# Weaving the attention of three mixers with projections and gates: one encoder kernel before and after

## The chip, the cores and the metric

The kernel runs on one core of a Trainium2 chip. The metric is the time of one execution in microseconds (us) on the device. A core has five engines that run side by side, each with a queue of its own that it works through in order: PE (TensorE, matrix products; its weight loads are shown as PEld), DVE (VectorE), ACT (ScalarE), POOL (GpSimd) and SP (SyncE, which here only issues DMAs). Matrix products go from SBUF into PSUM, and the other engines take them from there.

## The reference

Two layers work on 272 tokens (16 meta tokens and a grid of 4 rows by 64 columns) of width 1024. Each layer is a SwiGLU, a step with three mixers, and a second SwiGLU, all with residuals. The change concerns the step with the mixers:

```python
qa, ka, va, qb, kb, vb, qc, kc, vc, gates = jnp.split(n @ w_in, offsets, axis=-1)
...
oa = window_sink_attention(apply_rope(heads(qa, A_Q_HEADS), ang), apply_rope(heads(ka, A_KV_HEADS), ang),
                           heads(va, A_KV_HEADS), sink)
ob = neighbourhood_attention(heads(qb, B_HEADS), heads(kb, B_HEADS), heads(vb, B_HEADS), rpb)
qc = apply_axial_rope(rms_norm(heads(qc, C_Q_HEADS), qn), row, col)
kc = apply_axial_rope(rms_norm(heads(kc, C_KV_HEADS), kn), row, col)
oc = dense_block_attention(qc, kc, heads(vc, C_KV_HEADS))
branches = jnp.stack([oa, ob, oc], axis=2)
up = jnp.einsum('blnc,ncd->blnd', branches, w_branch)
g = jax.nn.sigmoid(gates.reshape(B, L, N_BRANCH, D_MODEL))
return jnp.sum(g * up, axis=2) @ w_out
```

So there are three attentions A, B and C with eight heads of 64 each (A within a window and with a sink logit, B within a neighbourhood on the grid, C over all tokens with normalised queries and keys), and each result goes through a branch matrix and is scaled by a gate, which is one more projection of the same normalised input. In the last layer only the 256 grid tokens are wanted, so that layer has no queries for the meta tokens.

## The kernel before

**Weights.** Activations lie transposed: 128 channels in the partitions, tokens along the free dimension. Every weight matrix comes in units of 512 x 256 numbers. SP issues the load of a unit into `raw` (four buffers), ACT rounds it into `hi` (L227), and DVE, or POOL for every third unit in the mixers, computes the rest `lo` (L228). `mm` (L271 to L273) multiplies each 128 x 128 block three times (hi by hi, hi by lo, lo by hi) into an accumulator `acc`, a PSUM tile of which there are two. A projection of 256 columns takes two units and 48 products; a branch takes one unit and 24.

**The mixers as written.** `mixer` writes its steps one behind the other: projections of B (values, keys, queries), then all of B's attention (`neighbourhood`), then A's keys and queries with their rotary turn (`rope_a`), then all of A's attention (`grouped` with br 0), then C's keys and queries (L721 to L763), then C's attention (`grouped` with br 2), then twelve gate steps in a loop (L769: four each for branch B, A and C), then the output projection.

**One attention.** An attention goes through two blocks of 128 queries, and each block through two halves of four heads. A half is a chain. PE computes four score tiles into PSUM tiles `s` (L468 or L604; three buffers). DVE adds masks and takes the maximum, and ACT the exponent (`scores`, L388 and L390, or L393 to L395). DVE normalises the four together (L407, L408, L481). PE turns the weights by transposes into `s` again (L487 or L612), ACT copies them out (L490 or L615), and after two halves `weighted` (L418, L423) multiplies them with the values into `pv`. After the two blocks, in the layer that has meta queries, the 16 meta tokens' queries go through the same chain once more (L502 to L534).

**The order on an engine.** The framework that builds the program orders each engine's instructions itself. The written order is their priority: an instruction that is ready and stands earlier goes first, and a later one may move ahead of it while it waits. A tile comes from a tag with so many buffers, and must wait until one is free. The tag `sm` of small tiles has 14 buffers. It serves A's and C's maxima `mx`, sums `den` and sink terms `e` (the `e` of `add_sinks` is first written at L400), and also C's norms: `rq`, `rqv` and `t24` of 24 columns and `sm` at L751. `rqv` is first written by the copies at L749, which take the sums of squares of C's queries out of the accumulator in which the projection of those queries lay (L739 and L746). Only after these copies, and in the first layer those of L757, is that accumulator free for another projection.

Of the kernel before, what the change touches and what calls it, by code (L numbers as in the profile page):

```python
# [17 lines left out]
D = 1024  # L18
# [73 lines left out]
def encoder_kernel(ctx: ExitStack, tc: tile.TileContext, x, meta_tokens, ffn1_norm, ffn1_w_in, ffn1_w_out,  # L92
# [359 lines left out]
    def grouped(br, q, kk, vt, oh, ol, masks, mask_m, sinks, sink_m, rq, meta_queries):  # L452

        v01, vm, v16 = v_prep(vt, meta_queries)
# [3 lines left out]
        for qi in range(2):  # L458
            pv = bank("pv")
            pm = sb.tile([128, 8, META], F32, name=nm("pm"), tag="pm", bufs=2)  # L460
            pmt = sb.tile([128, 128], F32, name=nm("pmt"), tag="pmt", bufs=2)
            both = []
            for half in range(2):
                p, mx, den = wide(), small(), small()
                for i in range(4):
                    t, g = 2 * half + i // 2, i % 2
                    s = bank("s", 3)[:, :T]
                    PE.matmul(s, q[g * HD:(g + 1) * HD, t, qi * 128:(qi + 1) * 128], kk[g * HD:(g + 1) * HD, :],  # L468
                              start=True, stop=True)
                    if rq is None:  # L470
                        scores(p, i, s, den, mx, masks[qi], nsink[:, 4 * g + t:4 * g + t + 1], None)
                    else:
                        c = qi * 8 + 2 * t + g
                        scores(p, i, s, den, mx, None, None, rq[:, c:c + 1])
                if rq is None:
                    e = small()
                    DVE.tensor_copy(e[:, :4].rearrange("p (t g) -> p t g", g=2),
                                    sinks.rearrange("p (g t) -> p t g", g=2)[:, 2 * half:2 * half + 2, :])
                    add_sinks(den, mx, e[:, :4], 4)
                normalise(p[:, :, :GRID], den)  # L480
                DVE.tensor_tensor(pm[:, 4 * half:4 * half + 4], p[:, :, GRID:],  # L481
                                  den[:, :4, None].to_broadcast([128, 4, META]), op=ALU.mult)
                for t2 in range(2):
                    pt = bank("s", 3)
                    for g in range(2):
                        for kt in range(2):
                            PE.transpose(pt[:, (2 * g + kt) * 128:(2 * g + kt + 1) * 128],  # L487
                                         p[:, 2 * t2 + g, kt * 128:(kt + 1) * 128], ident)
                    pts = sb.tile([128, 512], F32, name=nm("pts"), tag="pts", bufs=PTS)
                    ACT.copy(pts, pt)  # L490
                    both.append(pts)
            pt = bank("s", 3)
            PE.transpose(pt[:, :128], pm.rearrange("p a b -> p (a b)"), ident)
            DVE.tensor_copy(pmt, pt[:, :128])
            weighted(pv, vm, pmt, both, lambda t, g, kt, pts: (
                v01[:, kt, g * HD:(g + 1) * HD], pts[:, (2 * g + kt) * 128:(2 * g + kt + 1) * 128]))
            sl = (slice(None), slice(4 * br, 4 * br + 4), slice(qi * 128, (qi + 1) * 128))
            split(oh[sl], ol[sl], pv.rearrange("p (t q) -> p t q", t=4))
        if not meta_queries:
            return  # L500

        qm = sb.tile([128, 4, META], F32, name=nm("qm"), tag="qm", bufs=1)  # L502
        DVE.tensor_copy(qm, q[:, :, GRID:])
        qm = qm.rearrange("p t j -> p (t j)")
        s = bank("s", 3)[:, :T]
        for g in range(2):
            PE.matmul(s[g * HD:(g + 1) * HD, :], qm[g * HD:(g + 1) * HD, :], kk[g * HD:(g + 1) * HD, :],
                      start=True, stop=True)
        p = sb.tile([128, 1, T], F32, name=nm("pq"), tag="pq", bufs=1)
        den, mx = small(), small()  # L510
        if rq is None:
            nsink = small()
            DVE.tensor_scalar(nsink[:, :1], sink_m, -1.0, None, op0=ALU.mult)
        scores(p, 0, s, den, mx, mask_m, nsink[:, :1] if rq is None else None, None if rq is None else rq[:, 16:17])
        if rq is None:
            add_sinks(den, mx, sink_m, 1)
        normalise(p[:, 0:1, :], den)
# [32 lines left out]
    def neighbourhood(biases, q, kb, vb, oh, ol, meta_queries):  # L550
# [45 lines left out]
        for qi in range(2):  # L596
            pv = bank("pv")
            both = []
            for half in range(2):
                p, mx, den = wide(), small(), small()  # L600
                for i in range(4):
                    t, g = 2 * half + i // 2, i % 2
                    s = bank("s", 3)[:, :KB]
                    PE.matmul(s, q[g * HD:(g + 1) * HD, t, qi * 128:(qi + 1) * 128],  # L604
                              kb[g * HD:(g + 1) * HD, t, qi, :], start=True, stop=True)
                    scores(p, i, s, den, mx, biases[qi][:, 2 * t + g, :], 3.0e38, None)
                normalise(p[:, :, :KB], den)
                for t2 in range(2):
                    pt = bank("s", 3)
                    for g in range(2):  # L610
                        for kt in range(2):
                            PE.transpose(pt[:KH, (2 * g + kt) * 128:(2 * g + kt + 1) * 128],  # L612
                                         p[:, 2 * t2 + g, kt * KH:(kt + 1) * KH], ident)
                    pts = sb.tile([128, 512], F32, name=nm("pts"), tag="pts", bufs=PTS)
                    ACT.copy(pts[:KH].rearrange("p (b q) -> p b q", b=4), backwards(pt[:KH], 4))  # L615
                    both.append(pts)
# [4 lines left out]
            split(oh[sl], ol[sl], pv.rearrange("p (t q) -> p t q", t=4))  # L621


    def mixer(l, norm, nxt, last):
# [48 lines left out]
        neighbourhood(biases, qb, kb, vb, oh, ol, not last)  # L673


        tab = scr()
        DVE.tensor_tensor(tab[:, 0, :], C("cos_a"), r, op=ALU.mult)
        DVE.tensor_tensor(tab[:, 1, :], C("sin_a"), r, op=ALU.mult)
# [10 lines left out]
        qa = q_tile()  # L689
        a = proj(plain(w, 0, 8, A_KV))  # L690
        ka, va = kv_tile("k"), kv_tile("v")
        rope_a(ka[:, None, :], a[:, 0:1, :T], 1)
        DVE.tensor_tensor(va, a[:, 1, :T], r, op=ALU.mult)
        for half in range(2):
            a = proj(head_pairs(w, A_Q, half), n_out)
            rope_a(qa[:, 2 * half:2 * half + 2, :n_out], a[:, :, :n_out], 2)
        sink_m = None
        if not last:
            t8 = small()
            DVE.tensor_tensor(t8, sink[:, l, :], C("head_of"), op=ALU.mult)  # L700
            sink_m = small()
            DVE.tensor_reduce(sink_m[:, :1], t8, axis=AX, op=ALU.add)
            sink_m = sink_m[:, :1]
        grouped(0, qa, ka, va, oh, ol, (C("mask_a0"), C("mask_a1")), C("mask_am"), sink[:, l, :], sink_m, None,
                not last)


        rq = small((128, 24))
# [12 lines left out]
        a = proj(plain(w, 0, 8, C_KV))  # L721
        kc, vc = kv_tile("k"), kv_tile("v")
        u = scr()
        DVE.tensor_tensor(u[:, 0, :], a[:, 0, :T], r, op=ALU.mult)
        DVE.tensor_tensor(vc, a[:, 1, :T], r, op=ALU.mult)
        ACT.activation(u[:, 1, :], u[:, 0, :], AF.Square)
        for i in range(2):
            PE.matmul(a[:, i, T:T + 136], heads, u[:, 1, i * 136:(i + 1) * 136], start=True, stop=True)
        v2 = scr()
        rk = scr()  # L730
        DVE.tensor_scalar(v2[:, 0, :].rearrange("p (a b) -> p a b", a=2), a[:, :, T:T + 136], 1.0 / HD, EPS,
                          op0=ALU.mult, op1=ALU.add)
        rsqrt(rk[:, 0, :], v2[:, 0, :], v2[:, 1, :])
        rope_c(kc[:, None, :], u[:, 0:1, :], 2 + l, 1)
        DVE.tensor_tensor(kc, kc, rk[:, 0, :], op=ALU.mult)
        qc = q_tile()
        rqv = small((128, 24))
        for half in range(2):
# [9 lines left out]
            for qi in range(2):  # L748
                DVE.tensor_copy(rqv[:, qi * 8 + half * 4:qi * 8 + half * 4 + 4], a[:, 0, T + qi * 4:T + qi * 4 + 4])  # L749
            if not last:  # L750
                sm = small((128, 32))  # L751
                DVE.tensor_copy(sm.rearrange("p (t j) -> p t j", t=2), sq[:, :, GRID:])
                for g in range(2):
# [122 lines left out]
```

## Time and profile before

| what | value |
|---|---|
| time, median of three runs | 1374.4 us (1373.92 to 1376.08) |
| profiled execution: its time | 1374.38 us |
| profiled execution: first to last instruction | 1372.6 us |
| mean granted clock of PE | 0.985 |
| instructions shown as work on PE | 10703 |
| bytes read from memory | 214.78 MB |

The profile is of one execution. Its page gives busy times by engine, the busy shares in 40 slices, the chain of waits that ended last, and the costliest groups of instructions. Further views give stretches of the span with busy time and granted clock (windows), instructions in order of time (the timeline; "x8" is a run of eight like ones, and what stands in brackets at the end is the idle time of the engine just before it, with the instruction that ended it), and who waited for whom (waits). The first layer's mixers take about 225 to 460 us of the span, and the second's about 930 to 1130 us.

### The profile page before, as it was taken

To read this page: it belongs to the slowest core of one execution; us is meant where nothing else is said; L and a number is where in the kernel's file an instruction comes from. 1 tells how busy PE (TensorE), PEld (TensorE's weight loads), DVE (VectorE), ACT (ScalarE), POOL (GpSimd) and SP (SyncE) were. 2 spreads that over 40 slices of the span, in tenths; PEclk is the share of its full clock that TensorE was granted. 3 is DMA by queue.
4 is the path that set the end of the run, shared out by engine and by line. 5 is a ranking of instruction groups with operands and counts; after the bars stand their busy time and mean duration, and the time that the engine had idled before them with its cause. 6 is when DMAs were issued, how large, how long until landed. Compare 5 with 4: busy or idle time off the path is not lost.

```text
span 1372.6 us, 25976 instructions
## 1 busy us (share of the span) xinstructions
PE 1341.0 (98%) x10703; PEld 1295.2 (94%) x10703; DVE 898.5 (65%) x1326; ACT 651.6 (47%) x933; POOL 168.3 (12%) x99
## 2 busy tenths in 40 slices
PE   8999999997999999999999999999999999999997
PEld 8999999986789999999999999999888999999997
DVE  7665668687555577655677656676797556865663
ACT  6443444464454455434445434454565445543444
POOL 1000003231013330000000000022321242000000
PEclk9999999997899999999999999999999999999999
DMA  7665555432125666555555555555232466665652
GB/s 225 196 191 170 180 178 185 139 92 64 46 69 172 176 190 193 179 175 179 166 179 178 170 183 170 161 177 169 78 108 79 140 194 188 185 186 190 191 171 77
DMA packets 239010, 217.52 MB, mean 158 GB/s; under 512 B 24804, under 2 KB 237980, under 8 KB 238764
## 3 DMA queue, kind: packets, MB, share of 16 engines
q1 hardware_dynamic: 238540, 215.20, 51.1%
q8 instruction: 84, 1.38, 0.4%
q10 hardware_dynamic: 352, 0.66, 0.1%
q14 instruction: 34, 0.28, 0.1%
HBM read 214.78 MB, written 1.05 MB: 157 GB/s over the span
## 4 chain that ended last, share of the span: by engine, by line
PE 90%; DVE 6%; ACT 1%; issue 1%; DMA 0%; SPq 0%; DVEq 0%; ACTq 0%
PE acc L272 27%; PE acc L273 27%; PE acc L271 27%; PE s L468 2%; PE pv L423 2%; DVE p L408 1%; PE s L487 1%; PE s L604 1%; DVE lo L228 1%; PE pv L418 1%; PE s L612 1%; PE s L326 0%; DMA raw<-in_ffn_w_in_dram 0%; DVE xl L315 0%; DVE p L388 0%
## 5 line engine op out<-in xcount | busy, mean ns | idle before, releaser
L227 ACT CAST hi<-raw 128x1024 fp32r<-128x1024 f32 (+1 forms) x392 | 404.4, 1032 | 573.5 <-PE acc L272 413.3
L272 PE MATMUL acc<-xl,hi 128*128 128x272 f32 (+1 forms) x2176 | 627.5, 288 | 0.6 <-DVE xl L315 0.4
L273 PE MATMUL acc<-xh,lo 128*128 128x272 f32 (+1 forms) x2176 | 624.4, 287 | 0.7 <-DVE lo L228 0.7
L271 PE MATMUL acc<-xh,hi 128*128 128x272 f32 (+1 forms) x2176 | 624.2, 287 | 0.9 <-ACT xh L314 0.9
L228 DVE TENSOR_TENSOR lo<-raw,hi 128x1024 fp32r<-128x1024 f32 (+1 forms) x352 | 430.2, 1223 | 217.0 <-ACT hi L227 216.6
L271 PEld LDWEIGHTS acc<-xh,hi 128*128 128x128 f32 x2176 | 412.7, 190 | 6.1 <-issue 4.6
L272 PEld LDWEIGHTS acc<-xl,hi 128*128 128x128 f32 x2176 | 411.0, 189 | 5.4 <-issue 3.8
L273 PEld LDWEIGHTS acc<-xh,lo 128*128 128x128 f32 x2176 | 411.2, 189 | 4.1 <-issue 3.1
L272 PE MATMUL acc<-hl,hi 128*128 128x272 f32 (+1 forms) x704 | 201.9, 287 | 0.0
L273 PE MATMUL acc<-hh,lo 128*128 128x272 f32 (+1 forms) x704 | 201.1, 286 | 0.0
L271 PE MATMUL acc<-hh,hi 128*128 128x272 f32 (+1 forms) x704 | 200.4, 285 | 0.0
L228 POOL TENSOR_TENSOR lo<-raw,hi 128x1024 fp32r<-128x1024 f32 x40 | 97.9, 2447 | 307.7 <-ACT hi L227 307.7
L271 PEld LDWEIGHTS acc<-hh,hi 128*128 128x128 f32 x704 | 132.7, 189 | 0.1
L273 PEld LDWEIGHTS acc<-hh,lo 128*128 128x128 f32 x704 | 132.3, 188 | 0.0
L272 PEld LDWEIGHTS acc<-hl,hi 128*128 128x128 f32 x704 | 132.2, 188 | 0.0
L321 POOL TENSOR_TENSOR ss<-ss,scr 128x544 f32<-128x544 f32 (+1 forms) x12 | 17.5, 1460 | 600.6 <-ACT scr L318 600.6
L272 PE MATMUL acc<-ol,hi 128*128 128x272 f32 (+1 forms) x192 | 54.8, 286 | 0.0
L271 PE MATMUL acc<-oh,hi 128*128 128x272 f32 (+1 forms) x192 | 54.7, 285 | 0.0
L273 PE MATMUL acc<-oh,lo 128*128 128x272 f32 (+1 forms) x192 | 54.6, 285 | 0.0
L370 DVE TENSOR_TENSOR scr<-acc,scr 128x544 f32<-128x544 f32 (+1 forms) x40 | 28.7, 716 | 31.7 <-PE acc L273 31.6
L280 DVE SCALAR_TENSOR_TENSOR h<-acc,h 128x544 f32<-128x544 f32 (+1 forms) x40 | 28.5, 713 | 28.7 <-PE acc L273 28.5
L367 DVE TENSOR_TENSOR scr<-acc,rstd 128x544 f32<-128x544 f32 (+1 forms) x40 | 28.6, 715 | 26.2 <-PE acc L273 26.2
(228 smaller groups left out, 1322.6 us busy)
## 6 DMA issues: line engine op xcount, KB each, us to landing
raw<-in_ffn_w_in_dram SPq DMA_DIRECT2D x176, 512.0 KB, 3.6
raw<-in_ffn_w_out_dram SPq DMA_DIRECT2D x80, 512.0 KB, 3.4
raw<-in_w_in_dram SPq DMA_DIRECT2D x80, 512.0 KB, 3.7
raw<-in_w_in_dram SPq DMA_DIRECT2D x32, 256.0 KB, 3.2
raw<-in_w_branch_dram SPq DMA_DIRECT2D x32, 256.0 KB, 3.9
raw<-in_w_out_dram SPq DMA_DIRECT2D x16, 512.0 KB, 3.9
raw<-in_ffn_w_out_dram SPq DMA_DIRECT2D x16, 256.0 KB, 2.7
raw<-in_w_branch_dram SPq DMA_DIRECT2D x8, 512.0 KB, 3.4
```

Of the source, the lines that this page charges most:

```text
L227: ACT.copy(hi[:, :n], raw[:, :n])
L228: lo_engine().tensor_tensor(lo[:, :n], raw[:, :n], hi[:, :n].bitcast(F32), op=ALU.subtract)
L271: PE.matmul(o, a, rh, start=k == 0, stop=False)
L272: PE.matmul(o, a, rl, start=False, stop=False)
L273: PE.matmul(o, b, rh, start=False, stop=k == len(rows) - 1)
L280: DVE.scalar_tensor_tensor(hv, a[:, :, :n], 0.5, hv, op0=ALU.mult, op1=ALU.add)
L321: (DVE if j == 3 else POOL).tensor_tensor(ss, ss, dst, op=ALU.add)
L367: DVE.tensor_tensor(g, gate, rb, op=ALU.mult)
L370: DVE.tensor_tensor(g, up, g, op=ALU.mult)
L408: DVE.tensor_tensor(p, p, den[:, :n, None].to_broadcast([128, n, p.shape[2]]), op=ALU.mult)
L423: PE.matmul(pv[g * HD:(g + 1) * HD, t * 128:(t + 1) * 128], a, b, start=vm is None and kt == 0, stop=kt == 1 and (vm is None or t == 3))
L468: PE.matmul(s, q[g * HD:(g + 1) * HD, t, qi * 128:(qi + 1) * 128], kk[g * HD:(g + 1) * HD, :], start=True, stop=True)
```

## The change

`grouped` and `neighbourhood` become generators: after the four scores of a half they stop and let the caller write something else. Each half's turning of the weights, and after the second half the product with the values, is written behind the scores of the next half. The meta queries' scores are written ahead of the last turning. `mixer` puts its other steps into functions (`a_keys`, `a_queries`, `c_keys`, `c_queries`, `gated`) and `weave` writes one of them at each stop: A's keys and queries and C's keys between the halves of B, C's queries and gates of B between those of A, and the remaining gates of B and gates of A between those of C. The order of the projections among themselves, and so of the loads of their weights, is what it was. C's `rq`, `rqv` and `t24`, the meta squares `sqm` and A's `sinkm` get tiles of their own, outside the tag `sm`. The sums of squares of C's meta queries are taken once for both halves, and the copies at L749 are one for both query blocks.

```diff
+        def products(qi, half, pm):
+            p, mx, den = wide(), small(), small()
+            for i in range(4):
...
+            normalise(p[:, :, :GRID], den)
...
+        def turned(p):
...
+        def values(qi, pm, both):
...
+        last = None
+        for qi in range(2):
+            pm = sb.tile([128, 8, META], F32, name=nm("pm"), tag="pm", bufs=2)
+            done = []
+            for half in range(2):
+                p = products(qi, half, pm)
+                if last is not None:
+                    last()
+                yield
+                last = lambda p=p, qi=qi, half=half, pm=pm, done=done: (
+                    done.extend(turned(p)), values(qi, pm, done) if half else None)
+        if meta_queries:
+            p = meta_products()
+        last()
         if not meta_queries:
             return
...
+        yield
         pt = bank("s", 3)
...
-        rq = small((128, 24))
+        rq, rqv, t24 = (sb.tile([128, 24], F32, name=nm(x), tag=x, bufs=1) for x in ("rq", "rqv", "t24"))
+        sqm = sb.tile([128, 4, META], F32, name=nm("sqm"), tag="sqm", bufs=1)
...
-            for qi in range(2):
-                DVE.tensor_copy(rqv[:, qi * 8 + half * 4:qi * 8 + half * 4 + 4], a[:, 0, T + qi * 4:T + qi * 4 + 4])
+            DVE.tensor_copy(rqv[:, :16].rearrange("p (q h c) -> p q h c", q=2, h=2)[:, :, half, :],
+                            a[:, 0, T:T + 8].rearrange("p (q c) -> p q c", q=2))
             if not last:
-                sm = small((128, 32))
-                DVE.tensor_copy(sm.rearrange("p (t j) -> p t j", t=2), sq[:, :, GRID:])
-                for g in range(2):
-                    o = g * HD + half * 32
-                    PE.matmul(a[o:o + 32, 1, T:T + 1], sm[g * HD:(g + 1) * HD, :], ones[g * HD:(g + 1) * HD, :1],
-                              start=True, stop=True)
-                    DVE.tensor_copy(rqv[o:o + 32, 16:17], a[o:o + 32, 1, T:T + 1])
+                DVE.tensor_copy(sqm[:, 2 * half:2 * half + 2, :], sq[:, :, GRID:])
+                if half:
+                    for g in range(2):
+                        rows = slice(g * HD, (g + 1) * HD)
+                        PE.matmul(a[rows, 1, T:T + 1], sqm[rows].rearrange("p t j -> p (t j)"), ones[rows, :1],
+                                  start=True, stop=True)
+                    DVE.tensor_copy(rqv[:, 16:17], a[:, 1, T:T + 1])
...
+        def gated(b, mp):
+            if not tot:
+                tot.extend(qk(4, T) for _ in range(2))
+            if b == 2 and not halves:
+                halves.extend([qk(4, T, dt=F32R) for _ in range(2)] for _ in range(2))
...
+        def weave(attention, others):
+
+            for _ in attention:
+                if others:
+                    others.pop(0)()
+
+        others = [a_keys, lambda: a_queries(0), lambda: a_queries(1), c_keys]
+        weave(neighbourhood(biases, qb, kb, vb, oh, ol, not last), others)
+        others += [lambda: c_queries(0), lambda: c_queries(1)]
+        others += [lambda mp=mp: gated(1, mp) for mp in range(4)]
+        weave(mix_a(), others)
+        others += [lambda mp=mp: gated(0, mp) for mp in range(4)]
+        weave(mix_c(), others)
+        others += [lambda mp=mp: gated(2, mp) for mp in range(4)]
+        for work in others:
+            work()
```

More of the change, by code (lines that the diff above doesn't have):

```diff
@@ new lines, in turned @@
+        def turned(p):
+            both = []
+            for t2 in range(2):
+                pt = bank("s", 3)
+                for g in range(2):
+                    for kt in range(2):
+                        PE.transpose(pt[:, (2 * g + kt) * 128:(2 * g + kt + 1) * 128],
+                                     p[:, 2 * t2 + g, kt * 128:(kt + 1) * 128], ident)
+                pts = sb.tile([128, 512], F32, name=nm("pts"), tag="pts", bufs=PTS)
+                ACT.copy(pts, pt)
+                both.append(pts)
+            return both
@@ L499, in grouped @@
+        last()
         if not meta_queries:
             return
[L502 to L509, printed above, removed]
@@ L595, in neighbourhood @@
             split(oh[sl], ol[sl], pv[:, :4 * META].rearrange("p (t j) -> p t j", t=4))
-        for qi in range(2):
-            pv = bank("pv")
[L598 to L616, printed above, removed]
@@ new lines, in products @@
+        def products(qi, half):
+            p, mx, den = wide(), small(), small()
+            for i in range(4):
+                t, g = 2 * half + i // 2, i % 2
+                s = bank("s", 3)[:, :KB]
+                PE.matmul(s, q[g * HD:(g + 1) * HD, t, qi * 128:(qi + 1) * 128],
+                          kb[g * HD:(g + 1) * HD, t, qi, :], start=True, stop=True)
+                scores(p, i, s, den, mx, biases[qi][:, 2 * t + g, :], 3.0e38, None)
+            normalise(p[:, :, :KB], den)
+            return p
@@ new lines, in turned @@
+        def turned(p):
+            both = []
+            for t2 in range(2):
+                pt = bank("s", 3)
+                for g in range(2):
+                    for kt in range(2):
+                        PE.transpose(pt[:KH, (2 * g + kt) * 128:(2 * g + kt + 1) * 128],
+                                     p[:, 2 * t2 + g, kt * KH:(kt + 1) * KH], ident)
+                pts = sb.tile([128, 512], F32, name=nm("pts"), tag="pts", bufs=PTS)
+                ACT.copy(pts[:KH].rearrange("p (b q) -> p b q", b=4), backwards(pt[:KH], 4))
+                both.append(pts)
+            return both
@@ L617, in neighbourhood, with values @@
+        def values(qi, both):
+            pv = bank("pv")
             weighted(pv, None, None, both, lambda t, g, kt, pts: (
@@ L621, in neighbourhood @@
             split(oh[sl], ol[sl], pv.rearrange("p (t q) -> p t q", t=4))
+        last = None
+        for qi in range(2):
+            done = []
+            for half in range(2):
+                p = products(qi, half)
+                if last is not None:
+                    last()
+                yield
+                last = lambda p=p, qi=qi, half=half, done=done: (
+                    done.extend(turned(p)), values(qi, done) if half else None)
+        last()
     def mixer(l, norm, nxt, last):
@@ L672, in mixer @@
                                   op=ALU.mult)
[L673 to L678, printed above, removed]
+        tab = None
         def rope_a(dst, src, m):
@@ L719, in rope_c, with c_keys, c_queries @@
             DVE.tensor_tensor(dst, dst, t, op=ALU.add)
[L721 to L738, printed above, removed]
+        def c_keys():
+            a = proj(plain(w, 0, 8, C_KV))
+            u = scr()
+            DVE.tensor_tensor(u[:, 0, :], a[:, 0, :T], r, op=ALU.mult)
+            DVE.tensor_tensor(vc, a[:, 1, :T], r, op=ALU.mult)
+            ACT.activation(u[:, 1, :], u[:, 0, :], AF.Square)
+            for i in range(2):
+                PE.matmul(a[:, i, T:T + 136], heads, u[:, 1, i * 136:(i + 1) * 136], start=True, stop=True)
+            v2 = scr()
+            rk = scr()
+            DVE.tensor_scalar(v2[:, 0, :].rearrange("p (a b) -> p a b", a=2), a[:, :, T:T + 136], 1.0 / HD, EPS,
+                              op0=ALU.mult, op1=ALU.add)
+            rsqrt(rk[:, 0, :], v2[:, 0, :], v2[:, 1, :])
+            rope_c(kc[:, None, :], u[:, 0:1, :], 2 + l, 1)
+            DVE.tensor_tensor(kc, kc, rk[:, 0, :], op=ALU.mult)
+        def c_queries(half):
+            if not half:
+                qc[0] = q_tile()
             a = proj(head_pairs(w, C_Q, half), n_out)
@@ L758, in mixer @@
-            rope_c(qc[:, 2 * half:2 * half + 2, :n_out], u, l, 2)
-        nq = 16 if last else 17
-        t24 = small((128, 24))
-        DVE.tensor_scalar(rqv[:, :nq], rqv[:, :nq], 1.0 / HD, EPS, op0=ALU.mult, op1=ALU.add)
-        rsqrt(rq[:, :nq], rqv[:, :nq], t24[:, :nq])
-        DVE.tensor_scalar(rq[:, :nq], rq[:, :nq], 0.125, None, op0=ALU.mult)
-        grouped(2, qc, kc, vc, oh, ol, None, None, None, None, rq, not last)
-        tot = [qk(4, T) for _ in range(2)]
-        mh, ml = ([qk(4, T, dt=F32R) for _ in range(2)] for _ in range(2))
```

157 lines of the change are left out of this document (85 added, 72 removed).

## The prediction

> **What bounds the kernel now.** I read the page first, then PE's work by windows, then the timeline of the one stretch that stands out, then the waits.
>
> ```profile
> span 1372.6 us, 25976 instructions
> ...
> PE 1341.0 (98%) x10703; PEld 1295.2 (94%) x10703; DVE 898.5 (65%) x1326; ACT 651.6 (47%) x933; POOL 168.3 (12%) x99
> ...
> PEclk9999999997899999999999999999999999999999
> ...
> PE 90%; DVE 6%; ACT 1%; issue 1%; DMA 0%; SPq 0%; DVEq 0%; ACTq 0%
> ```
>
> PE is busy for 98% of the span and makes up 90% of the chain that ended last, so only what shortens PE's own time can count. The digits of the clock say where PE was slow: only in the tenth and eleventh slices, 309 to 377 us, which is the first layer's mixers. The windows go around that stretch, and then through the second layer's attention.
>
> ```profile
> 225.00:322.00 97.00, 95.82 (x767) 86.57 (x766) 73.63 (x193) 49.88 (x108) 26.09 (x17) 1.00 0.35 105
> 322.00:366.00 44.00, 33.35 (x182) 26.02 (x180) 22.99 (x74) 14.98 (x34) 4.58 (x2) 0.69 0.15 47
> 366.00:410.00 44.00, 41.66 (x321) 35.03 (x321) 27.60 (x56) 24.12 (x53) 7.45 (x3) 1.00 0.28 85
> ...
> 955.00:1080.00 125.00, 122.77 (x984) 105.23 (x982) 98.16 (x243) 76.02 (x173) 30.70 (x18) 1.00 0.32 97
> ```
>
> The columns are the stretch, its length, then busy time and instructions of PE, PEld, DVE, ACT and POOL, the granted clock, and the DMA share and rate. Before 322 us PE does 767 products in 97 us, 7.9 a microsecond; after 366 us 321 in 44, 7.3; in the second layer 984 in 125, 7.9. Between 322 and 366 us it does 182 in 44, 4.1 a microsecond, at a clock of 0.69, while DVE (23 us) and ACT (15 us) are half idle. So no engine bounds this stretch. The timeline of PE in it:
>
> ```profile
> 324.65 0.28 PE L273 MATMUL acc<-xh,lo 128*128 128x272 f32 x1
> 328.20 1.25 PE L487 MATMUL s<-cst,p 128*128 128x128 f32 x8 [3.27 <-DVE pm L481]
> 329.38 2.17 PE L468 MATMUL s<-k,qk 64*128 64x272 f32 x6
> 331.48 1.87 PE L746 MATMUL acc<-cst,scr 128*128 128x2 f32 x8
> 333.29 1.27 PE L468 MATMUL s<-k,qk 64*128 64x272 f32 x2
> 339.81 1.94 PE L487 MATMUL s<-cst,p 128*128 128x128 f32 x8 [5.25 <-DVE pm L481]
> 341.54 0.42 PE L493 MATMUL s<-cst,pm 128*128 128x128 f32 x1
> 341.89 1.17 PE L507 MATMUL s<-k,qm 64*64 64x272 f32 x2
> 342.98 2.07 PE L418 MATMUL pv<-pmt,vm 128*128 128x128 f32 x8
> 344.99 2.44 PE L423 MATMUL pv<-pts,v 128*64 128x128 f32 x32
> 347.36 0.67 PE L507 MATMUL s<-k,qm 64*64 64x272 f32 x2
> 349.63 0.22 PE L755 MATMUL acc<-ones,sm 64*32 64x1 f32 x2 [1.60 <-DVE sm L752]
> ...
> 355.48 0.59 PE L271 MATMUL acc<-xh,hi 128*128 128x272 f32 x1
> 355.87 0.43 PE L272 MATMUL acc<-xl,hi 128*128 128x272 f32 x1
> 356.10 0.43 PE L273 MATMUL acc<-xh,lo 128*128 128x272 f32 x1
> ```
>
> At 324.65 us the last product of C's query projection starts, and only at 355.48 us the next projection, the first gate's. For 31 us PE has nothing but A's attention, one chain of scores, exponents, turning and values, and the sums of C's squares (L746). It waits for the chain, and its clock drops. L746 between two rows of A's attention shows that the framework already moves C's work ahead of A's. Why then no gates? DVE's rows, with PE's L746 (315.75 and 1015.33) for comparison, the second layer below:
>
> ```profile
> 315.75 0.51 PE L746 MATMUL acc<-cst,scr 128*128 128x2 f32 x4
> ...
> 349.20 0.15 DVE L400 TENSOR_TENSOR sm<-sm,sm 128x1 f32<-128x1 f32 x1
> 349.26 0.22 DVE L749 COPY sm<-acc 128x4 f32<-128x4 f32 x2
> ...
> 351.93 0.17 DVE L757 COPY sm<-acc 32x1 f32<-32x1 f32 x1
> ```
> ```profile
> 1015.33 1.05 PE L746 MATMUL acc<-cst,scr 128*128 128x2 f32 x8
> ...
> 1022.91 0.15 DVE L400 TENSOR_TENSOR sm<-sm,sm 128x4 f32<-128x4 f32 x1
> 1022.99 0.22 DVE L749 COPY sm<-acc 128x4 f32<-128x4 f32 x2
> ```
>
> C's first sums are ready at 316 us, but L749 copies them out at 349.26, and L757 the last at 351.93; until then both accumulators belong to C's two query projections. In both layers L749 comes right behind an L400, which writes the last `e` of A: in the first layer that of A's meta queries (one column), in the second, where there are none, that of A's last half. I read this as the tag `sm` handing out its 14 buffers in written order: `rqv` stands behind all small tiles of A, so it has to wait until A's chain has taken its last one. In the second layer this comes early and costs nothing.
>
> **The change part by part.** The sum goes against the profiled execution's own time, 1374.38 us: 1372.6 us of span and 1.8 us around it; the median of the runs is 1374.40 us, the same.
>
> *Own tiles for `rq`, `rqv`, `t24`, `sqm`, and gates written between A's pieces.* `rqv` no longer waits for A's small tiles, an accumulator is free some 2 us after L746, and gate projections of 48 products each, with their branches of 24, can fill the stretch. What this is worth I work out in two ways. By counting: 182 products at 7.9 a microsecond take 23.0 us of the 44, at 7.3 they take 24.9, so 21.0 or 19.1 us go. By rows: the waits of 3.27, 5.25 and 1.60 us are 10.1 us. The clock of 0.69 over 44 us, if it knows only full and half, means 27.3 us at half; without the 5.25 us wait that lies in them some 22 us of work. What that work takes at full clock these rows show:
>
> ```profile
> 317.07 1.16 PE L418 MATMUL pv<-pmt,vm 128*128 128x128 f32 x8
> 318.16 1.97 PE L423 MATMUL pv<-pts,v 128*64 128x128 f32 x32
> ```
> ```profile
> 299.81 0.40 PE L272 MATMUL acc<-xl,hi 128*128 128x272 f32 x1
> 300.04 0.29 PE L273 MATMUL acc<-xh,lo 128*128 128x272 f32 x1
> 300.17 0.29 PE L271 MATMUL acc<-xh,hi 128*128 128x272 f32 x1
> ```
>
> L418 1.16 for 2.07 us, L423 1.97 for 2.44, a step of `acc` 0.13 (300.04 to 300.17) for 0.23 (355.87 to 356.10): about 0.6 of the time, so 22 us of work lose 8.8. Together 18.9 us. Of 18.9, 19.1 and 21.0 I take 19.5. [...]
>
> What hides the filling: DVE's work in 322 to 410 us, 22.99 + 27.60 = 50.6 us, must then fit into 68.5 us, 74%. It was 76% before 322 us (73.63 of 97) and 79% in the second layer (98.16 of 125), with PE at its full rate in both. DMA stands at 0.15 there. If DVE's cover were gone, PE would wait for `lo`, and the 7.3 row rather than the 7.9 one holds.
>
> *Turning behind the next scores.* PE gets the next half's scores before it must wait for the normalised weights, so it has work meanwhile, and DVE and ACT get it earlier.
>
> ```profile
> PE s L487 <- DVE pm L481: 9.6, 3, 5.3
> PE acc L755 <- DVE sm L752: 1.6, 1, 1.6
> PE s L468 <- ACT p L395: 1.1, 1, 1.1
> ```
>
> These are PE's longest waits in the first layer's mixers (total, times, longest). Beyond the stretch above, the turning waited 9.6 - 8.5 = 1.1 us and a score 1.1 us: at most 2.2 us to win there. Against it stands a new place to wait: the scores need a free `s` of three, which DVE or ACT frees, and behind a waiting score all of PE's queue stands, gates included. The one such wait seen took 1.1 us.
>
> *Finer weaving.* Each return from attention to a projection costs PE a step of 0.23 instead of 0.13 us (299.81 to 300.04, then 300.17), and the way in I estimate at the same, 0.2 us together. With one more such visit in each of the 24 halves (two layers, three mixers, four halves) that is 4.8 us; with fewer visits than now it would be a gain of the same kind. Between a gain of 2.2 and a loss of 4.8 us I take nothing, as the second layer, woven by the framework already, keeps 7.9 products a microsecond.
>
> *The rest.* Two fewer L749 copies, one for four at L757 and two products for four at L755 in the first layer's half are each 0.22 us or less on engines with slack: nothing. The steps moved ahead of attention (A's keys and queries, C's keys, the gates) keep their order, so their loads on SP, the thirds of `lo` on POOL and the accumulators come in the same sequence; none is moved past another load. The meta scores ahead of the last turning change no sum.
>
> The sum: 1374.4 - 19.5 = 1354.9, forecast 1355. What is late next is PE itself, at full rate.
>
> **The rivals.** *Half closed* (8%): the second accumulator. C's second query projection ends at 324.9 us, but its sums come from PE only at 333.3 (L746 from 331.48, 1.87 us), behind A's work on DVE and ACT. With one accumulator free, 48 products of 0.13 us last to about 331 us, and PE runs dry for some 3 us; the clock falls for half of its present time, 4.4 us. The gain shrinks to 12, the time is 1362. For it speaks that DVE is at 76% just before, against it that the second layer has the same order and no such gap.
>
> *The clock stays low* (4%): from 341.54 to 347.36 us PE hardly waits, and yet its rows are slow. If work of attention alone, not idle time, holds the clock down, and pieces still stand together, only the 10.1 us of waits go: 1364. [...] Against it: 955 to 1080 us holds four halves each of B, A and C at a clock of 1.00.
>
> *It does not do what it says* (4%): the framework orders by readiness, so the written order may matter little, and if L749 was late for another reason than its tag, the hole stays: 1374.
>
> *A wait for `s` in every half* (8%), the other side: if each of the 24 halves' scores held up PE's queue for the 1.1 us once seen, 26.4 us come back, and with the 19.5 won the time is 1381. From 19.5 / 24 = 0.8 us a half nothing is won, and from (19.5 + 2.7) / 24 = 0.9 us it is slower. Against it: other waits than the three of the stretch are few now.
>
> **How the numbers follow.** My forecast has 76%. Its own range is 1348 (21.0 and 2.2 us gained, and 3.4 us more by bringing 366 to 410 us to 7.9 products a microsecond: 321 / 7.9 = 40.6 us) to 1360 (18.9 gained, 4.8 lost). The range of 1348 to 1367 adds the two weaker gains and leaves out the hole that stays, the slower case and tails of the forecast, some 18%. About 0.2%, 2.7 us, is what a measurement of this kernel can tell from no change. Faster by more: the forecast and the two weaker gains, 88%. Within: the hole that stays, 4%. Slower: 8%.
>
> **What would show it.** In the profile after, the clock in the first layer's mixers is 1.00 throughout, no stretch of 31 us without a product into `acc` from `xh` or `oh` is left, PE does at least 7.3 products a microsecond there, the copies at L749's successor follow their sums by 1 to 4 us and not an L400, and the second layer's mixers keep their length within 3 us. If the gaps before the turning have gone but the clock is still under 0.9 in some window, the second rival holds. New waits of scores for DVE or ACT over 0.8 us a half, or a DVE busy for over 95% of 40 us with PE under 7 products a microsecond, would make the forecast wrong.

## The result and the profile after

| | median of four runs | lowest to highest |
|---|---|---|
| before | 1374.45 us | 1373.92 to 1376.08 |
| after | 1356.32 us | 1354.52 to 1358.10 |

The ratio is 0.9863, with a 95% interval of 0.9850 to 0.9876. The profiled execution of the kernel after took 1356.25 us, 1354.5 of them span. The forecast was 1355.

The page of the kernel after, the same lines as of before:

```profile
span 1354.5 us, 25919 instructions
...
PE 1330.5 (98%) x10699; PEld 1290.3 (95%) x10699; DVE 888.4 (66%) x1319; ACT 649.2 (48%) x933; POOL 164.7 (12%) x99
...
PEclk9999999999999999999999999999989999999998
...
PE 92%; DVE 5%; ACT 1%; issue 1%; DMA 0%; SPq 0%; DVEq 0%; ACTq 0%
```

The shares of the engines hardly moved: PE is at 98% again. What moved is the row of the clock. The 7 and the 8 in the tenth and eleventh slices are gone, and an 8 has come in the thirtieth, which is the second layer's mixers, and one in the last.

Where the 18 us went is read from the stages. The norm that follows the feed-forward part begins with the sums at L326. The first such row marks the start of the mixers, the next the start of the second SwiGLU. Before:

```profile
220.02 1.18 PE L326 MATMUL s<-ss,ones 128*128 128x272 f32 x4 [1.90 <-DVE ss L321]
522.26 1.08 PE L326 MATMUL s<-ss,ones 128*128 128x272 f32 x4
919.23 1.18 PE L326 MATMUL s<-ss,ones 128*128 128x272 f32 x4 [0.93 <-DVE ss L321]
1179.97 1.03 PE L326 MATMUL s<-ss,ones 128*128 128x256 f32 x4
```

And after:

```profile
220.51 1.18 PE L326 MATMUL s<-ss,ones 128*128 128x272 f32 x4 [1.91 <-DVE ss L321]
500.50 1.08 PE L326 MATMUL s<-ss,ones 128*128 128x272 f32 x4
897.47 1.18 PE L326 MATMUL s<-ss,ones 128*128 128x272 f32 x4 [0.94 <-DVE ss L321]
1161.85 1.03 PE L326 MATMUL s<-ss,ones 128*128 128x256 f32 x4
```

The first layer's mixers went from 302.2 us (522.26 - 220.02) to 280.0, so 22.2 us were won. The second layer's went from 260.7 to 264.4, so 3.7 us were lost. Between 500.50 and 897.47 the kernel after takes 397.0 us, and before between 522.26 and 919.23 also 397.0. So the change acts in the mixers alone, and with two signs.

The windows of the kernel after, over the same stretches as before (the second layer's moved by the 22 us that all starts earlier):

```profile
225.00:322.00 97.00, 94.99 (x755) 86.51 (x754) 75.78 (x192) 49.35 (x106) 30.12 (x19) 1.00 0.40 119
322.00:366.00 44.00, 43.80 (x359) 40.08 (x358) 26.91 (x73) 22.99 (x43) 7.18 (x3) 0.96 0.35 109
366.00:410.00 44.00, 44.00 (x330) 38.70 (x328) 26.46 (x58) 24.08 (x50) 9.86 (x5) 1.00 0.39 113
933.00:1058.00 125.00, 121.76 (x944) 108.08 (x944) 94.42 (x231) 72.79 (x162) 30.62 (x19) 0.96 0.36 110
```

From 322 to 366 us PE now does 359 products instead of 182, 8.2 a microsecond, and 330 in the 44 us behind it, 7.5. In the second layer 125 us hold 944 products where they held 984, at a clock of 0.96 where it was 1.00 (974 and 0.97 in a second profile of the same kernel, f1 below).

Why the stretch is filled is read from the sums of C's squares on PE and from their copies on DVE, both of the kernel after:

```profile
310.70 0.95 PE L798 MATMUL acc<-cst,scr 128*128 128x2 f32 x8
...
320.85 1.05 PE L798 MATMUL acc<-cst,scr 128*128 128x2 f32 x8
```
```profile
312.57 0.15 DVE L800 COPY rqv<-acc 128x8 f32<-128x8 f32 x1
...
323.25 0.15 DVE L800 COPY rqv<-acc 128x8 f32<-128x8 f32 x1
324.56 0.16 DVE L809 COPY rqv<-acc 128x1 f32<-128x1 f32 x1 [0.46 <-PE acc L807]
...
351.51 0.15 DVE L400 TENSOR_TENSOR sm<-sinkm,sm 128x1 f32<-128x1 f32 x1
```

L800, which took L749's place, copies 0.9 and 1.4 us behind the end of its sums (310.70 + 0.95, 320.85 + 1.05), and the last L400 of A stands 27 us behind the last of these copies. Before, the copy stood 0.06 us behind that L400. So the tie to A's last small tile is cut. But what cut it? The change does three things that could have done so: the tiles of their own, the late turning and the weaving. The experiments take them apart.

### The profile page after: what moved, and what is told of

Its sections match the earlier page's. It is cut to its first block, busy times and chain, and to the rows that moved or that the text cites. A ratio compares the mean times of both kernels' runs of the same rounds, so it can differ in the third digit from the quotient of the medians.

```text
span 1354.5 us, 25919 instructions
## 1 busy us (share of the span) xinstructions
PE 1330.5 (98%) x10699; PEld 1290.3 (95%) x10699; DVE 888.4 (66%) x1319; ACT 649.2 (48%) x933; POOL 164.7 (12%) x99
## 3 DMA queue, kind: packets, MB, share of 16 engines
HBM read 214.78 MB, written 1.05 MB: 159 GB/s over the span
## 4 chain that ended last, share of the span: by engine, by line
PE 92%; DVE 5%; ACT 1%; issue 1%; DMA 0%; SPq 0%; DVEq 0%; ACTq 0%
PE acc L272 28%; PE acc L271 28%; PE acc L273 28%; PE s L465 2%; PE pv L423 2%; DVE lo L228 1%; PE s L488 1%; PE s L627 1%; PE s L639 1%; ACT hi L227 1%; PE pv L418 1%; DMA raw<-in_ffn_w_in_dram 0%; PE s L326 0%; DVE xl L315 0%; DVE p L408 0%
## 6 DMA issues: line engine op xcount, KB each, us to landing
raw<-in_w_in_dram SPq DMA_DIRECT2D x32, 256.0 KB, 3.3
raw<-in_w_branch_dram SPq DMA_DIRECT2D x32, 256.0 KB, 3.8
raw<-in_ffn_w_out_dram SPq DMA_DIRECT2D x16, 256.0 KB, 2.7
```

## The experiments

All kernels below are timed against the kernel before on the same chip. They come from three chips, so kernels of different chips are compared by their ratios to it. "Woven" means that projections or gates are written between halves of an attention, "serial" that the steps stand one behind the other as before.

### The four corners: tiles, turning, weaving

**Own tiles alone** (e1). The kernel before, with nothing changed but the tiles:

```diff
-            sink_m = small()
+            sink_m = sb.tile([128, 8], F32, name=nm("sinkm"), tag="sinkm", bufs=1)
...
-        rq = small((128, 24))
+        rq, rqv, t24 = (sb.tile([128, 24], F32, name=nm(x), tag=x, bufs=1) for x in ("rq", "rqv", "t24"))
...
-                sm = small((128, 32))
+                sm = sb.tile([128, 32], F32, name=nm("sqm"), tag="sqm", bufs=2)
```

> The kernel before with rq, rqv, t24, the meta squares and A's sink term in tiles of their own; written order, turning and everything else as before. Theory T (the copies into rqv waited behind A's small tiles of the shared tag): the stretch without a projection, 324.7 to 355.5 us, closes by this alone and the time is 1354 to 1358. Theory W (gates must be written between A's pieces): the stretch stays, 1371 to 1375. In between, near 1362 to 1366, would say that each brings a part.

1356.45 us (1355.86 to 1358.42), ratio 0.9859 (0.9842 to 0.9875). The tiles alone bring what the whole change brings. DVE's rows of this kernel:

```profile
318.29 0.22 DVE L748 COPY rqv<-acc 128x4 f32<-128x4 f32 x2
...
347.58 0.16 DVE L400 TENSOR_TENSOR sm<-sinkm,sm 128x1 f32<-128x1 f32 x1
```

The copy (here L748) comes at 318.29, 29 us ahead of A's last L400. The first layer's mixers take 284.8 us, the second's 260.7 as before. So the reading of the tag holds: it was the order of handing out that kept the accumulators.

**Woven and turned late, but in the shared tag** (e2). The kernel after, with four tiles back in `sm`:

```diff
-                sink_m = sb.tile([128, 8], F32, name=nm("sinkm"), tag="sinkm", bufs=1)[:, :1]
+                sink_m = small()[:, :1]
...
-        rq, rqv, t24 = (sb.tile([128, 24], F32, name=nm(x), tag=x, bufs=1) for x in ("rq", "rqv", "t24"))
+        rq, rqv, t24 = (small((128, 24)) for x in ("rq", "rqv", "t24"))
```

> The kernel after with rq, rqv, t24 and A's sink term back in the shared tag sm of 14 buffers (the meta squares keep a tile of their own, for want of room); weaving and late turning as after. T: woven, C's queries are written behind A's first and second half, so that rqv has to wait only for the small tiles of these, and nothing of the gain is lost: 1355 to 1359. W says the same, 1355 to 1359. A time near 1374 would mean that only the tiles count, and the written order not at all.

1354.70 us (1354.39 to 1356.26), ratio 0.9846 (0.9830 to 0.9861), 281.7 us in the first layer's mixers. So beside the rest of the change the tiles bring nothing: what they do, another edit does too. Which one, DVE's rows of this kernel say:

```profile
312.76 0.17 DVE L800 COPY sm<-acc 128x8 f32<-128x8 f32 x1
...
326.19 0.15 DVE L809 COPY sm<-acc 128x1 f32<-128x1 f32 x1
...
353.12 0.15 DVE L400 TENSOR_TENSOR sm<-sm,sm 128x1 f32<-128x1 f32 x1
```

The copies come 27 us and more ahead of A's last L400, though all of them draw on the tag `sm`. Here C's queries are written between A's halves, so `rqv` takes its buffer ahead of A's later tiles: the woven order makes the cut.

**Woven, turned at once** (e4). The kernel after, with each half turned right behind its own scores, in both generators:

```diff
-                if last is not None:
-                    last()
+                done.extend(turned(p))
+                if half:
+                    values(qi, pm, done)
                 yield
-                last = lambda p=p, qi=qi, half=half, pm=pm, done=done: (
-                    done.extend(turned(p)), values(qi, pm, done) if half else None)
...
-        last()
```

> The kernel after with each half's turning written right behind its own scores again, and the values behind the second turning; own tiles and weaving as after. Prediction's step: late turning is worth between a gain of 2.2 us and a loss, taken at nothing: 1354 to 1359. Rival: late turning is what lets PE run on, and without it PE waits for normalised weights in each of 24 halves for 0.5 us or more: 1368 or more.

1367.75 us (1364.61 to 1369.61), ratio 0.9943 (0.9923 to 0.9962). That is 11 us above the kernel after: some three fifths of the gain are lost. Its windows and, for the first layer's mixers, its longest waits of PE (total, times, longest):

```profile
225.00:322.00 97.00, 93.79 (x724) 84.43 (x723) 70.36 (x182) 47.12 (x99) 27.98 (x18) 1.00 0.35 104
322.00:410.00 88.00, 85.61 (x656) 75.65 (x655) 55.09 (x129) 45.89 (x92) 14.61 (x7) 0.96 0.38 114
```
```profile
PE s L488 <- DVE pm L478: 2.2, 1, 2.2
PE acc L273 <- DVE lo L225: 1.1, 1, 1.1
PE s L488 <- DVE p L408: 0.9, 1, 0.9
```

724 and 656 products stand where the kernel after has 755 and, over 322 to 410 us as one stretch, 686: 61 fewer, some 8 us at 7.8 a microsecond. That is about the 8.1 us by which the first layer's mixers are longer (288.1 to 280.0). The second layer's differ little in the profiles (265.1 to 264.4). Two of the longest waits are the turning's (L488) for the normalised weights, 3.1 us together, and some 7 us at half clock follow the longer one; the kernel after has no such wait here. So this is where the late turning earns most of its time. The profiled execution (1364.61 us) is the fastest of this kernel, so it shows 8 of the 11 us.

**Not woven, turned late** (e5, and once more as f2). The kernel after, with its steps written as before:

```diff
-        weave(neighbourhood(biases, qb, kb, vb, oh, ol, not last), others)
...
+        for _ in neighbourhood(biases, qb, kb, vb, oh, ol, not last):
+            pass
+        a_keys()
+        a_queries(0)
+        a_queries(1)
+        for _ in mix_a():
+            pass
+        c_keys()
+        c_queries(0)
+        c_queries(1)
+        for _ in mix_c():
+            pass
+        for b in (1, 0, 2):
+            for mp in range(4):
+                gated(b, mp)
```

> The kernel after with nothing woven: written order of the steps as before (A's projections, A, C's projections, C, all gates), with own tiles and late turning as after. T: weaving is not needed, 1352 to 1358, and the wait of 2.3 us for C's squares in the second layer with its 10 us of half clock, which the woven order brought, may go with it. W: the stretch is open again, 1368 to 1375.

1354.37 us (1352.70 to 1357.78), ratio 0.9844 (0.9822 to 0.9866). To tell a difference of 2 us from none, the kernel after and this one ran again side by side:

> The changed kernel as it is, beside the next three on one chip. Ratio to before as measured, 0.986 within 0.002.

> The kernel of e5_not_woven_late_turn again. Theory V (weaving costs PE time, late turning wins it back): 0.984 or less, some 2 to 4 us faster than the changed kernel. Rival (the difference of the single profiles, 1350.9 against 1354.5 us, is scatter of the clock): within 1 us of the changed kernel.

1354.95 us (0.9849, 0.9834 to 0.9863) for the kernel after and 1355.02 us (0.9851, 0.9831 to 0.9870) unwoven. So the seeming gain was scatter, and the weaving as a whole brings nothing that these runs can tell.

Together the four kernels with tiles of their own make a square:

| | turned at once | turned late |
|---|---|---|
| serial | 1356.45 (e1) | 1354.37, 1355.02 (e5, f2) |
| woven | 1367.75 (e4) | 1356.32, 1354.95 (after, f1) |

Weaving costs 11 us where the weights are turned at once and nothing where they are turned late. By the ratios the late turning is worth 11 to 13 us in the woven order and 1 to 2 in the serial one, where the intervals overlap, so that it may be nothing (e1 also keeps the copies and products apart that the change joins). Inside the change the two cancel.

**Late turning alone, in the shared tag** (g1). Own tiles suffice, and in e2 the woven order did. The question left was whether the hole comes back with neither. This is the unwoven kernel (e5) with the four tiles back in `sm`, the same edit as e2's:

> The kernel of e5 (steps written one behind the other, late turning) with rq, rqv, t24 and A's sink term back in the shared tag of 14 buffers. Theory T (rqv is handed out only behind all of A's small tiles): late turning alone doesn't cure it, the first layer again has a stretch of about 25 to 30 us without a projection, 1366 to 1374. Rival: the meta scores written ahead of the last turning, and A's chain shortened by late turning, let A's last small tile come so early that little is lost: 1354 to 1360.

1353.63 us (1350.49 to 1355.15), ratio 0.9840 (0.9822 to 0.9858). The hole is closed here too, without own tiles and without weaving; the theory that it would come back fell. DVE's rows show why:

```profile
324.82 0.13 DVE L400 TENSOR_TENSOR sm<-sm,sm 128x1 f32<-128x1 f32 x1
...
334.09 0.16 DVE L800 COPY sm<-acc 128x8 f32<-128x8 f32 x1
```

The last L400 of A now comes at 324.82 us, some 24 us earlier than before (349.20). The meta queries' scores are written ahead of A's last turning, and each half's scores ahead of the turning in front of them. C's first sums end at 333.23 us, so A takes its last small tile before C's sums want theirs, and the order of the tag costs nothing. Own tiles alone (e1) or late turning alone (g1) is enough. That late turning is not what closed the hole in e2 follows from its rows, where A's last L400 stands at 353.12 us, no earlier than before. But no kernel has the weaving alone, with the shared tag and turned at once.

### What of the weaving costs, and what pays

**Only gates woven** (f3, and again as g3). Steps serial, own tiles, late turning, and the gates of B and A two at a time between the halves of C:

```diff
-        weave(mix_c(), others)
+        others = [lambda b=b, mp=mp: gated(b, mp) for b in (1, 0) for mp in range(4)]
+        for _ in mix_c():
+            for _ in range(2):
+                if others:
+                    others.pop(0)()
```

> The kernel of e5 with the gates of B and A, two at a time, written between the halves of C, and no projection between those of B or A. If the cost of weaving lies with the gates: as slow as the changed kernel, some 1356. If it lies with A's and C's projections, whose work on DVE (rotary turns, squares, key norms) then goes ahead of the masks and maxima of A and B: as fast as e5, some 1353.

> The kernel of f3_gates_woven_only again, for its interval: ratio to before 0.983 within 0.002, faster than the changed kernel by 2 to 4 us.

1351.45 us (0.9828, 0.9809 to 0.9847) and 1352.95 us (0.9838, 0.9823 to 0.9854). By the ratios that is 1 to 3 us under the kernel after in f1, with intervals that overlap its own (0.9834 to 0.9863): a hint and not more.

**Only projections woven** (f4). A's keys and queries and C's keys between the halves of B, C's queries between those of A, all gates behind C:

```diff
-        weave(mix_a(), others)
...
+        weave(mix_a(), [lambda: c_queries(0), lambda: c_queries(1)])
+        for _ in mix_c():
+            pass
+        for b in (1, 0, 2):
+            for mp in range(4):
+                gated(b, mp)
```

> The kernel of e5 with A's keys and queries and C's keys between the halves of B and C's queries between those of A, and all gates behind C. The other half of the same question: some 1356 with PE's wait for C's squares or A's scores near 990 us if the projections carry the cost, some 1353 if the gates do.

1357.99 us (1357.55 to 1360.65), ratio 0.9874 (0.9859 to 0.9889), apart from f3's interval, 6 us above f3 and 5 above g3 by the ratios. But f4 and f3 differ in two things, the projections and the gates. The kernel with neither woven (f2, 0.9851) and the one with both (f1, 0.9849) lie between, on the same chip:

| | gates behind C | gates woven |
|---|---|---|
| projections serial | 1355.02 (f2) | 1351.45 (f3) |
| projections woven | 1357.99 (f4) | 1354.95 (f1) |

By the medians woven projections cost some 3 us and woven gates bring some 3, either way round, and the two cancel. Each single step is smaller than the intervals are wide, and those of neighbours in the table overlap; only f4 and f3 are clear of each other. So the two prices are likely and not shown. Where the cost falls isn't shown: in single profiles the mixers of the two layers take 283.4 and 265.5 us in f4, 278.2 and 263.2 in f2, 281.9 and 261.9 in f3, and the profiled executions of f3 and f4 are the slowest of their four.

**Only gates woven, turned at once** (g4). f3 with e4's edit:

> The kernel of f3 with each half turned right behind its own scores. If turning at once costs 11 us only together with projections woven into A and B (e4): 1353 to 1357. If late turning is worth that much in any order: 1362 or more.

1354.79 us (1354.47 to 1356.85), ratio 0.9856 (0.9840 to 0.9873; 0.9838 was g3's beside it, 0.9840 g1's). Turning at once costs some 2 us here, again with intervals that overlap, as in the serial order. e4, which has projections between the halves too, stands at 0.9943, 12 us higher. So among these kernels the large cost comes only with them.

### What the second layer lost

The chain behind the clock of 0.96 in the second layer of the kernel after, in order of time over all engines:

```profile
985.31 3.13 POOL L228 TENSOR_TENSOR lo<-raw,hi 128x1024 fp32r<-128x1024 f32 x1 [0.20 <-ACT hi L227]
986.12 2.41 DVE L478 TENSOR_TENSOR pm<-p,sm 128x64 f32<-128x64 f32 x1
...
993.26 0.66 DVE L793 TENSOR_TENSOR scr<-acc,rstd 128x512 f32<-128x512 f32 x1
...
994.01 0.63 ACT L794 ACTIVATE scr<-scr 128x512 f32<-128x512 f32 x1 [1.53 <-DVE scr L793]
994.69 1.37 PE L798 MATMUL acc<-cst,scr 128*128 128x2 f32 x8 [2.28 <-ACT scr L794]
...
994.96 0.21 DVE L478 TENSOR_TENSOR pm<-p,sm 128x64 f32<-128x64 f32 x1
```
```profile
995.30:1005.50 10.20, 10.20 (x44) 9.27 (x45) 6.45 (x23) 5.17 (x13) 1.33 (x1) 0.50 0.19 56
1005.50:1010.00 4.50, 4.50 (x55) 4.38 (x55) 2.75 (x8) 2.66 (x4) 0.42 (x1) 1.00 0.26 86
```

A small DVE instruction, L478, takes 2.41 us at 986.12 and 0.21 us at 994.96. The long one ends at 988.53, 0.09 us behind POOL's `lo`. From there on DVE works without a gap, so what it lost it passes on: DVE scales C's queries (L793) at 993.26, ACT squares them (L794) behind it, PE waits 2.28 us for the squares (L798), and then works for 10.2 us at half clock. 44 products in 10.2 us, where 7.9 a microsecond would be 81: 37 products, 4.7 us. With the wait that is more than the 3.7 us that this layer lost. It is not all that the layer can lose: unwoven (e5, f2) there is no such wait for squares, and the layer still takes 263.1 and 263.2 us, with a wait of 1.60 us for POOL's rotary turn (L465 behind L726) and 3.4 us at half clock.

Over both mixers of the kernel after, 28 DVE instructions that overlap one of POOL take at least 0.3 us longer than the shortest of their line and shape, 33.1 us in all; in the kernel before there are 35 with 39.5 us. So such hold-ups are not new with the change. The last experiment takes the `lo` away from POOL.

**All `lo` on DVE** (g2). The kernel after, with POOL's share of the rounding rest given back to DVE:

```diff
-        return POOL if in_mixer[0] and unit_no[0] % 3 == 0 else DVE
+        return DVE
...
-                (DVE if g else POOL).tensor_tensor(lv[:, :, :, g], rv[:, :, g], hv[:, :, :, g].bitcast(F32), op=ALU.subtract)
+                DVE.tensor_tensor(lv[:, :, :, g], rv[:, :, g], hv[:, :, :, g].bitcast(F32), op=ALU.subtract)
```

> The changed kernel with all of the weights' lo parts in the mixers on DVE, none on POOL. Theory P (DVE's instructions of 2.4 us that usually take 0.2 to 0.7 stand beside POOL's lo, so POOL holds them up, and through them the squares and PE): the long DVE instructions and PE's wait of 2.3 us for the squares go, 1350 to 1354. Rival D (DVE is the fuller engine there, and some 49 us of lo more on it cost more than the hold-ups): 1358 or more.

1343.24 us (1342.90 to 1343.81), ratio 0.9768 (0.9753 to 0.9782): 11 to 13 us under the kernel after by the ratios, and 32 under the kernel before on the same chip (1375.7). It beats both, although it gives more work to the fuller engine. Its page and windows:

```profile
span 1341.2 us, 25864 instructions
...
PE 1324.4 (99%) x10699; PEld 1285.3 (96%) x10699; DVE 917.9 (68%) x1375; ACT 648.2 (48%) x933; POOL 47.2 (4%) x43
```
```profile
225.00:322.00 97.00, 95.80 (x763) 86.94 (x763) 78.54 (x207) 49.75 (x106) 8.42 (x6) 1.00 0.38 115
322.00:410.00 88.00, 87.77 (x696) 79.05 (x695) 61.81 (x137) 47.75 (x96) 2.70 (x2) 1.00 0.40 120
933.00:1058.00 125.00, 124.88 (x1028) 111.46 (x1027) 102.61 (x246) 75.09 (x164) 8.12 (x7) 1.00 0.38 115
```

DVE got 56 instructions more and stands at 82% of the second layer's window (102.61 of 125), yet PE is idle for 0.12 us of it, does 1028 products where the kernel after does 944, and the clock is 1.00 in all three (this kernel runs 5 us ahead by then, so the stretch is not quite the same work). The held-up instructions are down to 12, with 11.8 us. The mixers take 276.7 and 256.0 us, 11.7 less than after. This shows that POOL's `lo` is the source. It is not that a `lo` of POOL comes too late for PE: in the mixers of the kernel after none of PE's waits over 0.2 us is for a `lo`. By which of the waits each microsecond came back isn't taken apart further, nor what POOL's own other steps gain.

## Why the prediction was right, and where it was not

**The hole.** Predicted: 19.5 us, from the copies' tie to A's last small tile. The tie was the cause, since cutting it alone (e1) gives 1.4% of 1376.8, 19.4 us, and 17.4 us in the profiled first layer (302.2 less 284.8); within the whole change that layer won 22.2. The counting was of the right kind: 359 less 182 products in 322 to 366 us are 177, and at 7.9 a microsecond 22.4 us. The way by rows put 27.3 us at half clock, on the condition that the clock knows only full and half. In the profiles of before and after all of its records stand at 1.00 or 0.50, and before has 17.1 and 10.2 us at 0.50 in this stretch. The tiles, though, were not the only cut, as the prediction had it: the woven order makes it too, by handing out `rqv` ahead of A's later tiles (e2), and in the serial order so does the late turning, by bringing A's last L400 forward by 24 us (g1). Gates written between A's pieces, which the prediction put beside the tiles, were not needed (e1).

**Turning behind the next scores, taken at nothing.** The bound of 2.2 us of gain holds in the serial order, where it is worth 1 to 2 us. Beside woven projections it is worth about 12. The bound was read from the waits of before, where no projection stood between the halves, and the edit beside it made new waits for it to hide.

**Finer weaving, taken at nothing, at most 4.8 us of loss.** All the weaving costs 11 us when turned at once (e1 to e4), more than twice the bound; turned late it costs nothing that shows. The two terms are not independent, and the prediction priced them as if they were. That together they came to about nothing (e1 1356.45, after 1356.32 us) was luck: the one hides what the other costs. The price of 0.2 us for each visit was not what counted: the loss lay in waits and in the clock that followed them.

**The second layer within 3 us.** It grew by 3.7 us in the profile and by 2.1 in the second one (262.8, f1). In it stands a wait of 2.28 us with half clock behind it, which the prediction had not seen, since no such wait was in the second layer before. The half clock lasts 10.2 us in the one profile and 6.8 in the other.

**The clock at 1.00 throughout the first layer.** It was 0.96 from 322 to 366 us. That is 3.4 us at half clock, which began 2.6 us behind the end of one wait, of 1.68 us, for a score's tile that DVE's maximum frees (L465 behind L388). DVE was late there because POOL's `lo` stood beside its L770, which takes 0.7 us elsewhere (in g2, without that `lo`, both the long L770 and the wait are gone):

```profile
314.82 2.41 POOL L228 TENSOR_TENSOR lo<-raw,hi 128x1024 fp32r<-128x1024 f32 x1 [2.26 <-ACT hi L227]
...
315.14 2.67 DVE L770 TENSOR_TENSOR qk<-qk,scr 128x544 f32<-128x544 f32 x1
...
320.20 0.72 PE L465 MATMUL s<-k,qk 64*128 64x272 f32 x2 [1.68 <-DVE sm L388]
```

The stretch at half clock:

```profile
322.80:326.20 3.40, 3.40 (x19) 3.13 (x18) 2.94 (x13) 0.61 (x2) 0.00 (x0) 0.50 0.00 1
```

19 products where 27 would fit, 1 us. This is not the half-closed hole of the first rival: that was to be a lack of accumulators, and what PE waited for was an `s`. Nor was the clock of the kernel before under 1.00 only about the waits of 3.27 and 5.25 us: it was at 1.00 again from 346.0 to 352.8 us and then at 0.50 for 10.2 us, 3 us behind the wait of 1.60.

**DVE as the cover.** Over 322 to 410 us it stood at 61% (53.4 of 88), below the 74% worked out, and it did not bound PE. That it was held by POOL, and that this was worth 11 to 13 us, appeared nowhere in the prediction.

**The rivals.** A wait for `s` in every half did not come: from 225 us to the end of the first layer's mixers PE waited 2.2 us for scores to find an `s`, in three waits, the longest the 1.68. "Does nothing" fell with e1. "The clock stays low" fell with the row of 366 to 410 us at 1.00, with attention and gates mixed.

## What to carry to other kernels

When an engine does half its usual number of instructions for some 30 us while nothing is full, look for the copy that waits, and see whether it follows the last use of a shared tag by others and not its own producer; a tile that is first written late should not share a tag with a long chain. Before pricing an edit as nothing because the waits of before are short, ask which other edit of the same change makes new waits for it to hide, and build the two apart. Moving a step to an idle engine can cost more than it saves, as here, where all `lo` on DVE is 11 to 13 us faster than a share of them on POOL (g2): compare the length of the busy engine's instructions with and without that neighbour.

## What the runs showed of the hardware

**Half clock stood behind some short waits of PE, and not behind others.** In the kernel after, waits of 1.68 and 2.28 us were followed by 3.4 and 10.2 us at 0.50; in other kernels here a wait of 2.24 us (e4) was followed by some 7 us, one of 1.48 us (e2) by 3.4 us. The length of the wait does not decide it. At the start of the first layer's mixers PE waits 1.90 or 1.91 us for the same sums (L326) in every profile but g2's: in e2, f3, f4, g1, g3 and g4 3.4 us at half clock began within 1.3 us, in the other seven none did. A wait of 2.62 us in e2 was followed by no drop (1.00 from 1003.8 to 1012 us). The stretches at half clock in the mixers are 3.4, 6.8 or 10.2 us long, and 17.1 in the kernel before, whole multiples of 3.41 (3.41 and 10.24 in the clock's records of after, 17.07 and 10.24 in those of before). What decides between a drop and none is not shown. A wait of 2.28 us cost 2.28 and 4.7 us more in one execution, so a layer's length in a single profile can differ by a microsecond or two between executions of one kernel (264.4 and 262.8 for the second layer in after and f1).

**Some of DVE's instructions took longer beside POOL's.** POOL's `lo` takes 3.13 us at 985.31, and L478 beside it 2.41 instead of 0.21; the `lo` at 314.82 takes 2.41, and L770 beside it 2.67 instead of 0.7. L478 ends 0.09 us behind POOL's `lo` and L770 0.58 behind it, neither by more than its own time (0.21 and 0.7 us), as if each had done its work only then; what held them until then is not shown. Not every instruction is held: in both mixers of the kernel after 193 of DVE's overlap one of POOL, and 28 of these take the 0.3 us or more longer. Of those that overlap none of POOL not one does. With POOL's `lo` gone the kernel is 11 to 13 us faster (g2).
